# Turning v and the keys by 32x32 squares on VectorE and ScalarE instead of on TensorE, and spreading the gates' row by DMA

## The chip, the cores and the metric

The kernel runs on one core of one Trainium2 chip. The engines that matter here are TensorE (in the profile PE, with its weight loads as PEld), VectorE (DVE), ScalarE (ACT), GpSimd (POOL) and SyncE (SP), which issues most of the transfers. Each engine works through its own list of instructions in the order in which the program put them, and waits for the others by semaphores.

The metric is the device time of one execution in microseconds. The kernel before takes 1883.01 us as the median of three runs (1882.06 to 1885.18).

## What is computed

One decoder layer for 256 tokens of width 2048, in float32. Two token mixers run side by side and are merged by gates, then come a cross-attention into 256 memory tokens and a gated feed-forward part with a short causal convolution. Cut to the parts that matter here:

```
proj = h @ w_in                                   # all inputs of both mixers, and the gates
q, k, v, o, ir, fr = split(mlstm part)            # mLSTM: 4 heads, chunks of 64
r, kr, vr, wl, al, gl = split(rwkv part, shifted) # RWKV-7: 16 heads of 64

# mLSTM, per head: weights of token s for token t from the gates' running sums
b    = cumsum(logf);  dmat = b_t - b_s + i_s  (s <= t)
m_t  = max(b_t + m, max_s dmat);  dexp = exp(dmat - m_t)
s    = (q @ k.T) * dexp;  h = (s @ v) / max(|sum s|, exp(-m_t))

# RWKV-7, per head and token:
S = S * diag(w) - (S kk) (kk a).T + v k.T ;   y = S r

x = x + norm(merge(mLSTM, RWKV) @ w_out)
x = x + norm(cross_attention(norm(x), norm(mem)))
x = x + norm(gelu(conv(u)_gate) * conv(u)_up @ w_down)
```

## The kernel before

Most of the time goes into products of activations with weights that stream from memory. Each float32 weight chunk (128 x 1024 elements, 512 KB) is loaded by SP and split into a high part `wh` by ScalarE (line 410) and a low part `wl` by VectorE (line 432, `raw - wh`). Activations are split in the same way (`hh`, `hl`), and each product is three matrix instructions: high with high, high with low, low with high. They are all recorded by the helper `mm` at line 188. A block of kind "fm" gives features on the partitions and 256 tokens in the free dimension (results named `fm`); a block of kind "tm" gives tokens on the partitions (named `tm`). `wh` and `wl` have four buffers each, and the raw chunks three.

`run` (the loop over all blocks) writes the instruction lists by hand. While it emits the products of one chunk it calls `side.half()` after every half chunk, which is 12 products of an fm block. At each such step the class `Spread` lets side work emit one piece: first the evacuation of the last block (`bulk`), then background tasks (`back`), each only while a running budget for VectorE and ScalarE is positive, and then the chains, which emit a piece every so many steps (their `chain` number) whatever the bulk does. A generator's `yield` ends a piece, so an empty `yield` waits for one step. What is emitted earlier stands earlier in each engine's list.

The blocks come in this order: small weights and gates, r, k, v, q and k of the mLSTM, its v and o, the branch gates, the two branches, the mixer's output, the cross-attention, and the feed-forward part.

Three places are touched by the change.

**v.** `v_evac` (two blocks, `hf` 0 and 1) writes v with features on the partitions into `vT`. The recurrence also needs it with tokens on the partitions, in `vt`. After four empty steps TensorE turns four squares of 128x128 into a PSUM bank (line 939), ScalarE copies the bank to `vt`, and this happens twice per block. Then `start_rwkv` may start the recurrence, and `bonus(hf)` is added to the background tasks.

**Keys.** `rwkv(hf)` runs the recurrence for half of the heads in four chunks of 64 tokens. Both halves advance together, one piece every three steps. In the first three chunks TensorE turns four squares of the keys `BK` into a PSUM bank (line 981), and ScalarE copies the bank into `bkt`. `bkt` is read at the end of the chunk by the state's update (`Tn`). The pieces of a chunk are: the turning; the Gram products (`gram`) with two masks by VectorE; the inverse blocks and the copies of v; `lv1` and `X`; `lv2`; `U`; then `Tn` and `Y`. `inverses` is the background task that prepares `M["cmt"]` before the recurrence can start: Gram products (`gramA`) by TensorE and some sixty small VectorE operations.

**The gates' row.** `gates` computes the gates' running values with four heads on four partitions. One row of 256 values per head, `R[6]`, must be known on all 128 partitions. It is split into a high and a low part, and TensorE multiplies each with a column of the 4x4 identity `id4` into the PSUM tile `gbc`: two groups of four products, one per pair of heads. VectorE clamps the differences into `pw` (24 operations), and ScalarE takes the exponential.

`x_tokens`, much later, already turns the residual for the output by VectorE (32x32 squares) and ScalarE, in the way the change now uses for v.

Of the kernel before, what the change touches and what calls it, by code (L numbers as in the profile page):

```python
# [15 lines left out]
P = 128  # L16
# [136 lines left out]
def _layer(ctx, tc, nc, d, dbg):  # L153
# [12 lines left out]
    def T2(name, shape=None, dt=F32):  # L166
        return mp.tile(shape or [P, 2, S], dt, tag="T2", bufs=6, name=name)

# [43 lines left out]
    E2 = [slice(0, 64), slice(64, 128)]  # L212
    mhalf = cp.tile([P, 16], F32, name="mhalf")
    pool.memset(mhalf, -0.5)
# [359 lines left out]
    flip = [0]  # L574

    def PR():
        flip[0] += 1
        if flip[0] % 2:
            M["pr"] = C("pr", "bg1", [P, 2, 2, S])
        return M["pr"][:, 1 - flip[0] % 2]  # L580
# [73 lines left out]

    id4 = cp.tile([4, 4], F32R, name="id4")

    def gates():

        act.copy(id4, con[0:4, 0:4])
        RT = M["rows"]  # L660
# [72 lines left out]
        M["pw"] = pw  # L733
        g2 = T2("g2", dt=F32R)
        split(g2[0:4, 0], g2[0:4, 1], R[6])
        for _ in range(6):
            yield
        for h2 in range(2):
            q = aux("gbc", [P, 2, S])
            for j in range(2):  # L740
                sel = id4[:, h2 * 2 + j:h2 * 2 + j + 1].broadcast_to((4, P))
                mm(q[:, j], sel, g2[0:4, 0], stop=False)
                mm(q[:, j], sel, g2[0:4, 1], start=False)
            for j in range(2):
                h = h2 * 2 + j
                for (jt, dq), ci in CI.items():
                    o = jt * 256 + dq * 64 - jt * 128
                    dve.tensor_scalar(pw[:, h, o:o + 64], q[:, j, dq * 64:(dq + 1) * 64], cols[:, ci, h:h + 1], 0.0,
                                      op0=ALU.subtract, op1=ALU.max)
                yield  # L750
# [171 lines left out]
    def v_evac(hf):  # L922
        def gen(ps):
            if hf == 0:
                M["vT"], M["vt"] = U("vT"), U("vt", [P, 2, 1024])
            for g in range(2):
                p0 = hf * 4 + g * 2
                pr = PR()
                dve.tensor_mul(pr, ps[g], bc(st0.rb, 2))
                yield  # L930
                for j in range(2):
                    shiftmix(M["vT"][:, p0 + j], pr[:, j], 16 + p0 + j)
                yield
            for _ in range(4):
                yield
            for t in range(2):
                q = aux("vt", [P, 4, 128])
                for j in range(4):
                    pe.transpose(q[:, j], M["vT"][:, hf * 4 + j, t * P:(t + 1) * P], ident)
                act.copy(M["vt"][:, t, hf * 512:(hf + 1) * 512], q)  # L940
                yield
            M["v", hf] = True
            start_rwkv()
            tasks["bon", hf] = side.add(bonus(hf), back=True)
        return gen

    def bonus(hf):
# [11 lines left out]
    def rwkv(hf):  # L959
# [6 lines left out]
        def heads():  # L966
            for j in range(4):
                for e in range(2):
                    yield j, e

        ysb = None
        for c in range(4):
# [5 lines left out]
            if c < 3:  # L978
                q = aux("bkt", [P, 4, 128])
                for j in range(4):  # L980
                    pe.transpose(q[:, j], flat(BK[:, p0 + j, c]), ident)
                act.copy(bkt, q)
                yield
            au = C("au", f"au{hf}", [P, 2, 2, 4, 64])
# [4 lines left out]
            for e in range(2):  # L989
                dve.tensor_mul(ab[:, e], qs[e][:, :, 0:64], bc(sm, 4))  # L990
                dve.tensor_mul(gr[:, e], qs[e][:, :, 64:128], bc(im, 4))
                yield

# [6 lines left out]
            for e in range(2):  # L1000
                act.copy(uv[E2[1 - e], e], v[:, e])
            yield

# [9 lines left out]
            if c:  # L1013
# [651 lines left out]
    def x_tokens():  # L1665

        M["xt"] = []
        for f in range(4):
            if f % 2 == 0:
                M["xt"].append(U("xt", [P, 2, 1024]))  # L1670
            q = C("xq", f"au{f % 2}", [P, 4, 2, 4, 32])
            flat = q.rearrange("p k t b i -> p (k t b i)")
            for i in range(2):
                v = M["xr"][f // 2][:, f % 2 * 4 + i * 2:f % 2 * 4 + i * 2 + 2]
                dve.transpose(flat[:, i * 512:(i + 1) * 512], v.rearrange("p k s -> p (k s)"))
                yield
            o = M["xt"][f // 2][:, :, f % 2 * 512:f % 2 * 512 + 512].rearrange("p t (k b i) -> p t k b i", k=4, b=4)
            for b in range(4):
                for c in range(4):
                    act.copy(o[b * 32:b * 32 + 32, :, :, c], q[c * 32:c * 32 + 32, :, :, b].rearrange("p k t i -> p t k i"))  # L1680
                    if c % 2:
                        yield

# [157 lines left out]
```

## Time and profile before

| What | Value |
|---|---|
| median of three runs | 1883.01 us (1882.06 to 1885.18) |
| the profiled execution, its own time | 1882.86 us |
| its span from first to last instruction | 1881.1 us |
| TensorE busy | 1867.8 us, 99% |
| VectorE busy | 1313.9 us, 70% |
| ScalarE busy | 1035.0 us, 55% |
| granted TensorE clock | 0.997 over the span |
| transposes of v, on TensorE | 16, from 156.0 to 181.6 us |
| transposes of keys, on TensorE | 24, from 262.3 to 390.5 us |
| products of the gates' row | 8, from 83.4 to 87.5 us |

In a row of a group the figures after the bar are the busy time of all its instructions and the mean time of one in ns, and after the second bar the idle time of the engine before them. In a row of the timeline the first two figures are start and length in us, and equal neighbours are merged (x4). A matrix instruction's length is longer than the distance to the next one, because they are pipelined, so prices on TensorE are read from start to start. The profiled execution lies 1.8 us above its span.

### The profile page before, as it was taken

The numbers are of one execution on the slowest core, as the hardware profiler recorded it, in microseconds if no ns is written. First come the engines' busy times: TensorE is split into PE (matmuls) and PEld (weight loads), VectorE is DVE, ScalarE is ACT, GpSimd is POOL, SyncE is SP. The second block draws the span as 40 slices with busy tenths as digits, with TensorE's granted clock in tenths as the row PEclk, the third lists the DMA queues.
The fourth block names the chain that finished last, engine by engine and source line by source line (L and its number), as shares of the span: only waits on it lengthen the run. The fifth ranks groups of instructions, "written<-read, shape, count | busy, mean of one in ns | idle before, by whom it ended". The sixth has DMA issues, their size and how long they took to land.

```text
span 1881.1 us, 36660 instructions
## 1 busy us (share of the span) xinstructions
PE 1867.8 (99%) x15038; PEld 1774.5 (94%) x15038; DVE 1313.9 (70%) x1957; ACT 1035.0 (55%) x1619; POOL 30.6 (2%) x53
## 2 busy tenths in 40 slices
PE   9999999999999999999999999999999999999998
PEld 9999988999999999899999999999999998888886
DVE  6879985765765767777877666777666675556555
ACT  6677355554544655666565555564445555545453
POOL 0000000100100000000000000000000000000000
PEclk9999999999999999999999999999999999999999
DMA  7655554354556664545555566555655556555554
GB/s 252 196 175 181 167 177 146 110 175 146 182 175 206 237 234 163 176 163 180 197 196 192 199 194 198 194 191 191 195 198 193 196 191 216 195 192 196 193 190 154
DMA packets 97912, 352.73 MB, mean 188 GB/s; under 512 B 11056, under 2 KB 11312, under 8 KB 97360
## 3 DMA queue, kind: packets, MB, share of 16 engines
q1 hardware_dynamic: 96496, 348.07, 56.2%
q8 instruction: 117, 1.92, 0.4%
q0 software_dynamic: 384, 1.18, 0.3%
q10 hardware_dynamic: 864, 1.15, 0.2%
q14 instruction: 51, 0.42, 0.1%
HBM read 347.73 MB, written 2.10 MB: 186 GB/s over the span
## 4 chain that ended last, share of the span: by engine, by line
PE 95%; DVE 3%; issue 1%; ACT 1%; DMA 0%; POOL 0%; SPq 0%; DVEq 0%; POOLq 0%; ACTq 0%
PE fm L188 66%; PE tm L188 24%; DVE wl L432 1%; PE gram L188 0%; PE Y L188 0%; DVE ql L66 0%; ACT wh L410 0%; PE lv L188 0%; DMA wsm<-in_w_sm_dram 0%; DVE z L66 0%; PE num L188 0%; DVE hl L66 0%; PE X L188 0%; PE zwa L188 0%; PE U L188 0%
## 5 line engine op out<-in xcount | busy, mean ns | idle before, releaser
L432 DVE TENSOR_TENSOR wl<-raw,wh 128x1024 fp32r<-128x1024 f32 (+2 forms) x756 | 789.3, 1059 | 427.4 <-ACT wh L410 424.3
L410 ACT CAST wh<-raw 128x1024 fp32r<-128x1024 f32 (+2 forms) x756 | 679.8, 916 | 520.7 <-PE fm L188 335.0
L188 PE MATMUL fm<-fh,wl 128*128 128x256 f32 x2048 | 566.3, 277 | 0.5 <-DVE wl L432 0.4
L188 PE MATMUL fm<-fh,wh 128*128 128x256 f32 x2048 | 566.3, 277 | 0.1
L188 PE MATMUL fm<-fl,wh 128*128 128x256 f32 x2048 | 565.0, 276 | 0.0
L188 PEld LDWEIGHTS fm<-fh,wl 128*128 128x128 f32 x2048 | 385.0, 188 | 1.0 <-DVE wl L432 1.0
L188 PEld LDWEIGHTS fm<-fh,wh 128*128 128x128 f32 x2048 | 384.9, 188 | 0.4 <-ACT fh L66 0.4
L188 PEld LDWEIGHTS fm<-fl,wh 128*128 128x128 f32 x2048 | 384.5, 188 | 0.0
L188 PE MATMUL tm<-wh,as 128*128 128x512 f32 x1024 | 315.1, 389 | 0.0
L188 PE MATMUL fm<-hh,wh 128*128 128x256 f32 x1072 | 302.0, 282 | 1.4 <-ACT wh L421 1.4
L188 PE MATMUL fm<-hh,wl 128*128 128x256 f32 x1072 | 298.3, 278 | 0.1
L188 PE MATMUL fm<-hl,wh 128*128 128x256 f32 x1072 | 298.2, 278 | 0.0
L188 PEld LDWEIGHTS tm<-wh,as 128*128 128x128 f32 x1024 | 192.1, 188 | 39.8
L188 PEld LDWEIGHTS fm<-hh,wh 128*128 128x128 f32 x1072 | 202.4, 189 | 3.4 <-ACT hh L66 1.5
L188 PEld LDWEIGHTS fm<-hl,wh 128*128 128x128 f32 x1072 | 202.4, 189 | 0.2
L188 PEld LDWEIGHTS fm<-hh,wl 128*128 128x128 f32 x1072 | 202.3, 189 | 0.3 <-DVE wl L422 0.3
L188 PE MATMUL tm<-wl,as 128*128 128x512 f32 x512 | 199.2, 389 | 0.0
L188 PEld LDWEIGHTS tm<-wl,as 128*128 128x128 f32 x512 | 96.1, 188 | 20.0
L66 ACT CAST as<-ac 128x256 fp32r<-128x256 f32 x128 | 45.6, 404 | 113.5 <-PE tm L188 113.5
L66 DVE TENSOR_TENSOR as<-ac,as 128x256 fp32r<-128x256 f32 x128 | 48.6, 421 | 62.2 <-ACT as L66 62.2
L188 PE MATMUL fm<-mgh,wh 128*128 128x256 f32 x256 | 71.0, 277 | 0.0
L188 PE MATMUL fm<-mgh,wl 128*128 128x256 f32 x256 | 70.9, 277 | 0.0
(361 smaller groups left out, 2156.1 us busy)
## 6 DMA issues: line engine op xcount, KB each, us to landing
raw<-in_w_fu_dram SPq DMA_DIRECT2D x256, 512.0 KB, 4.2
raw<-in_w_in_dram SPq DMA_DIRECT2D x160, 512.0 KB, 3.7
raw<-in_w_fd_dram SPq DMA_DIRECT2D x128, 512.0 KB, 4.0
raw<-in_w_br_dram SPq DMA_DIRECT2D x32, 512.0 KB, 3.9
raw<-in_w_mo_dram SPq DMA_DIRECT2D x32, 512.0 KB, 4.1
raw<-in_w_xk_dram SPq DMA_DIRECT2D x8, 512.0 KB, 4.3
raw<-in_w_xq_dram SPq DMA_DIRECT2D x8, 512.0 KB, 3.6
raw<-in_w_xv_dram SPq DMA_DIRECT2D x8, 512.0 KB, 3.9
```

Of the source, the lines that this page charges most:

```text
L66: return f(out, *a, **k)
L188: pe.matmul(out, lhsT, rhs, start=start, stop=stop, skip_group_check=True)
L410: nc.scalar.copy(h, v)
L432: nc.vector.tensor_sub(l, v, h)
```

## The change

- v: `v_evac` ends after its shift and hands over to a new chain `v_tokens(hf)` (a piece every two steps). For each pair of feature tiles, VectorE transposes 128 x 512 elements in squares of 32x32 into a small tile `vq` (one instruction per pair), and ScalarE carries the squares to their places in `vt`: 16 copies of 32 partitions per pair, each with 128 elements per partition. `v_tokens` then marks v as ready, starts the recurrence if it may, and adds `bonus`.
- Keys: in each of the first three chunks, `keys` does the same for `BK`: one transpose of 128 x 512 by VectorE, then 16 copies by ScalarE. The transpose is emitted with the chunk's first piece. The copies follow three at a time per half in four pieces, and the rest at `lv2`. The piece that only did the turning is gone, so a chunk has one piece less.
- The gates' row: no split, no `id4` and no products. Four transfers on POOL's queue copy `R[6]` of each head from its one partition to 128 partitions of `gb` in SBUF. VectorE clamps from there, after eight empty steps instead of six.
- `x_tokens` uses the new helper `turned`, with the same instructions as before. The T2 tiles have seven buffers instead of six, and `mhalf` has 24 columns instead of 16.

```diff
-        return mp.tile(shape or [P, 2, S], dt, tag="T2", bufs=6, name=name)
+        return mp.tile(shape or [P, 2, S], dt, tag="T2", bufs=7, name=name)
...
-    mhalf = cp.tile([P, 16], F32, name="mhalf")
+    mhalf = cp.tile([P, 24], F32, name="mhalf")
...
+    def turned(q, v, o):
+        n = v.shape[1]
+        flat = q.rearrange("p k t b i -> p (k t b i)")
+        for k in range(0, n, 2):
+            dve.transpose(flat[:, k * S:(k + 2) * S], v[:, k:k + 2].rearrange("p k s -> p (k s)"))
+            yield
+        o = o.rearrange("p t (k b i) -> p t k b i", k=n, b=4)
+        for b in range(4):
+            for c in range(4):
+                act.copy(o[b * 32:b * 32 + 32, :, :, c], q[c * 32:c * 32 + 32, :, :, b].rearrange("p k t i -> p t k i"))
+                if c % 2:
+                    yield
...
-    id4 = cp.tile([4, 4], F32R, name="id4")
...
-        act.copy(id4, con[0:4, 0:4])
...
-        g2 = T2("g2", dt=F32R)
-        split(g2[0:4, 0], g2[0:4, 1], R[6])
-        for _ in range(6):
+        gb = C("gb", "au1", [P, 4, S])
+        for h in range(4):
+            pool.dma_start(gb[:, h], R[6][h:h + 1].unsqueeze(1).broadcast_to((1, P, S)))
+        for _ in range(8):
             yield
         for h2 in range(2):
-            q = aux("gbc", [P, 2, S])
-            for j in range(2):
-                sel = id4[:, h2 * 2 + j:h2 * 2 + j + 1].broadcast_to((4, P))
-                mm(q[:, j], sel, g2[0:4, 0], stop=False)
-                mm(q[:, j], sel, g2[0:4, 1], start=False)
...
-                    dve.tensor_scalar(pw[:, h, o:o + 64], q[:, j, dq * 64:(dq + 1) * 64], cols[:, ci, h:h + 1], 0.0,
+                    dve.tensor_scalar(pw[:, h, o:o + 64], gb[:, h, dq * 64:(dq + 1) * 64], cols[:, ci, h:h + 1], 0.0,
...
-            for _ in range(4):
-                yield
-            for t in range(2):
-                q = aux("vt", [P, 4, 128])
-                for j in range(4):
-                    pe.transpose(q[:, j], M["vT"][:, hf * 4 + j, t * P:(t + 1) * P], ident)
-                act.copy(M["vt"][:, t, hf * 512:(hf + 1) * 512], q)
-                yield
-            M["v", hf] = True
-            start_rwkv()
-            tasks["bon", hf] = side.add(bonus(hf), back=True)
+            side.add(v_tokens(hf), chain=2)
         return gen
+
+    def v_tokens(hf):
+        for p0 in (hf * 4, hf * 4 + 2):
+            yield from turned(T2("vq", [P, 2, 2, 4, 32]), M["vT"][:, p0:p0 + 2], M["vt"][:, :, p0 * P:p0 * P + 256])
+        M["v", hf] = True
+        start_rwkv()
+        tasks["bon", hf] = side.add(bonus(hf), back=True)
...
+        def keys(o, v):
+            q = T2("bq", [P, 4, 4, 32])
+            dve.transpose(q.rearrange("p j b i -> p j (b i)"), v.rearrange("p j s t -> p j (s t)"))
+            yield
+            for b in range(4):
+                for a in range(4):
+                    act.copy(o[b * 32:b * 32 + 32, :, a * 32:a * 32 + 32], q[a * 32:a * 32 + 32, :, b])
+                    yield
...
             if c < 3:
-                q = aux("bkt", [P, 4, 128])
-                for j in range(4):
-                    pe.transpose(q[:, j], flat(BK[:, p0 + j, c]), ident)
-                act.copy(bkt, q)
-                yield
+                turn = keys(bkt, BK[:, p0:p0 + 4, c])
+                next(turn)
+            else:
+                turn = iter(())
...
                 dve.tensor_mul(gr[:, e], qs[e][:, :, 64:128], bc(im, 4))
+                for _ in zip(range(3), turn):
+                    pass
                 yield
...
                 act.copy(uv[E2[1 - e], e], v[:, e])
+            for _ in zip(range(3), turn):
+                pass
             yield
...
                     dve.tensor_add(uv[E2[e], e], uv[E2[e], e], q[E2[e]])
+            for _ in zip(range(3), turn):
+                pass
             yield
...
                 dve.tensor_copy(mt[r, :, 32:64], q[r])
+            for _ in turn:
+                pass
             yield
```

More of the change, by code (lines that the diff above doesn't have):

```diff
@@ L1671, in x_tokens @@
             q = C("xq", f"au{f % 2}", [P, 4, 2, 4, 32])
[L1672 to L1675, printed above, removed]
+            v = M["xr"][f // 2][:, f % 2 * 4:f % 2 * 4 + 4]
+            o = M["xt"][f // 2][:, :, f % 2 * 512:f % 2 * 512 + 512]
+            for _ in turned(q, v, o):
                 yield
[L1677 to L1682, printed above, removed]
     def load_gain():
```

## The prediction

> **What bounds the kernel.** I read the page's parts 1, 2 and 4 first, then TensorE's waits, then the timeline around each operation that the change removes, and last the lead that VectorE has over TensorE in that stretch. From the page, and from the view of the waits (who waited for whom: us, times, longest):
>
> ```profile
> span 1881.1 us, 36660 instructions
> PE 1867.8 (99%) x15038; PEld 1774.5 (94%) x15038; DVE 1313.9 (70%) x1957; ACT 1035.0 (55%) x1619; POOL 30.6 (2%) x53
> ...
> PE 95%; DVE 3%; issue 1%; ACT 1%; DMA 0%; POOL 0%; SPq 0%; DVEq 0%; POOLq 0%; ACTq 0%
> ...
> PE fm L188 <- ACT wh L421: 1.4, 1, 1.4
> ...
> PE fm L188 <- DVE wl L432: 0.4, 1, 0.4
> ```
>
> TensorE is busy 99% of the span, is 95% of the chain that ended last, and waits for other engines some microseconds in all. So a microsecond taken off TensorE's queue is a microsecond off the kernel, provided that no engine that feeds it becomes late.
>
> **What TensorE loses.** The products go out one every 0.113 us in the feature-major blocks (155.82, 155.93 below) and one every 0.227 us in the token-major ones. Timeline of TensorE at a group of each kind that the change removes:
>
> ```profile
> 155.82 0.28 PE L188 MATMUL fm<-hl,wh 128*128 128x256 f32 x1
> 155.93 0.28 PE L188 MATMUL fm<-hh,wl 128*128 128x256 f32 x1
> 156.05 0.60 PE L939 MATMUL vt<-con,vT 128*128 128x128 f32 x4
> 156.41 0.37 PE L188 MATMUL fm<-hh,wh 128*128 128x256 f32 x1
> 156.62 0.28 PE L188 MATMUL fm<-hl,wh 128*128 128x256 f32 x1
> ```
>
> ```profile
> 262.31 0.39 PE L188 MATMUL tm<-wl,hh 128*128 128x512 f32 x1
> 262.55 1.03 PE L981 MATMUL bkt<-con,BK 128*128 128x128 f32 x8
> 263.33 0.48 PE L188 MATMUL tm<-wh,hh 128*128 128x512 f32 x1
> 263.65 0.40 PE L188 MATMUL tm<-wh,hl 128*128 128x512 f32 x1
> ```
>
> ```profile
> 83.20 0.28 PE L188 MATMUL fm<-hh,wl 128*128 128x256 f32 x1
> 83.41 0.74 PE L188 MATMUL gbc<-g,id 4*128 4x256 f32 x4
> 84.08 0.39 PE L188 MATMUL fm<-hh,wh 128*128 128x256 f32 x1
> 84.30 0.28 PE L188 MATMUL fm<-hl,wh 128*128 128x256 f32 x1
> ```
>
> ```profile
> L981 PE MATMUL bkt<-con,BK 128*128 128x128 f32 x24 | 3.1, 272 | 0.0
> ...
> L939 PE MATMUL vt<-con,vT 128*128 128x128 f32 x16 | 2.4, 273 | 0.0
> ...
> L188 PE MATMUL gbc<-g,id 4*128 4x256 f32 x8 | 1.5, 303 | 0.0
> ```
>
> The price of a group is the time from the product before it to the second product after it, less two steps. Four squares of v: 156.62 - 155.93 - 2 x 0.113 = 0.46, and 16/4 = 4 groups give 1.85. Eight squares of keys: 263.65 - 262.31 - 2 x 0.227 = 0.89, and 24/8 = 3 groups give 2.67. Four products of the gates' row: 84.30 - 83.20 - 2 x 0.113 = 0.87, and 2 groups give 1.75. Together **6.3 us** leave TensorE, all on the path.
>
> **What the other engines gain.** Groups with their shapes (busy, mean ns of one):
>
> ```profile
> L66 DVE STREAM_TRANSPOSE xq<-xr 128x512 f32<-128x512 f32 x8 | 5.6, 704 | 0.0
> ...
> L66 DVE TENSOR_SCALAR pw<-gbc,cols 128x64 f32<-128x64 f32 x24 | 4.8, 279 | 0.0
> ```
>
> ```profile
> L66 ACT COPY xt<-xq 32x256 f32<-32x256 f32 x64 | 25.8, 403 | 1.0
> ...
> L66 ACT ACT_TABLE_LOAD x4 | 5.1, 1283 | 2.9 <-PEq L1833 1.7 <-DVE tg L66 1.3
> ...
> L66 ACT COPY bg<-bkt 128x512 f32<-128x512 f32 x6 | 3.2, 588 | 2.4 <-PE bkt L981 2.3
> ...
> L66 ACT COPY vt<-vt 128x512 f32<-128x512 f32 x4 | 2.4, 588 | 3.4 <-PE vt L939 3.4
> L66 ACT COPY m<-lv 128x128 f32<-128x128 f32 x8 | 2.1, 265 | 5.3 <-PE lv L188 5.1
> ```
>
> VectorE: four transposes of 128x512 for v, six for the keys, at 704 ns: 7.0 us. Its 24 clamps of the gates change their source from PSUM to SBUF; I count them at the same 279 ns.
>
> ScalarE: 4 x 16 + 6 x 16 = 160 copies of 32 partitions x 128 elements. No row has that shape. Below it lies 0.265 us (m, as many elements, PSUM to SBUF), above it 0.403 us (xt, the same helper's copies with twice the elements). I take 0.30, since the difference of those two is mostly 128 more elements. 160 x 0.30 = 48 us, less the ten evacuations that go (10 x 0.588 = 5.9): about 42 us more on an engine that is busy 55%. The order of the changed program also holds nine table loads instead of seven, as the gates' exponentials now fall between two groups of sigmoids: 2 x 1.28 = 2.6 us more. The keys are wanted within their chunk, v only when the inverses are done. `x_tokens` issues through the new helper what it issued before; the seventh T2 buffer, the wider `mhalf` and the missing `id4` move small tiles only, and the order shows the products on the same operands: nothing for these.
>
> [...] By the rows, four squares cost 0.46 us of TensorE and 0.588 of ScalarE before, and 0.70 of VectorE and 16 x 0.30 = 4.8 of ScalarE after. [...] By the rows the freed engine is the one that bounds, and the sum starts from the 6.3 us.
>
> **VectorE's lead, where v is turned.** Busy time by stretch (PE, PEld, DVE, ACT, POOL, clock, DMA share, GB/s), then two weights' low parts and the products that first use them:
>
> ```profile
> 150.00:200.00 50.00, 50.00 (x459) 49.80 (x458) 46.66 (x73) 33.62 (x55) 6.46 (x8) 1.00 0.56 178
> 200.00:250.00 50.00, 50.00 (x371) 44.25 (x371) 45.44 (x81) 18.19 (x19) 0.00 (x0) 1.00 0.53 169
> 250.00:300.00 50.00, 50.00 (x367) 41.17 (x365) 36.06 (x61) 28.84 (x40) 0.00 (x0) 1.00 0.52 160
> ```
>
> ```profile
> 219.13 1.22 DVE L432 TENSOR_TENSOR wl<-raw,wh 128x1024 fp32r<-128x1024 f32 x1
> ...
> 224.91 0.39 PE L188 MATMUL tm<-wl,hh 128*128 128x512 f32 x1
> ```
>
> ```profile
> 259.13 1.23 DVE L432 TENSOR_TENSOR wl<-raw,wh 128x1024 fp32r<-128x1024 f32 x1 [0.70 <-ACT wh L410]
> ...
> 263.88 0.39 PE L188 MATMUL tm<-wl,hh 128*128 128x512 f32 x1
> ```
>
> VectorE is idle for only 7.9 of the 100 us from 150 to 250. The two tiles are ready 224.91 - 220.35 = 4.6 us and 263.88 - 260.36 = 3.5 us ahead of their use; every weight tile stands in VectorE's queue behind whatever was issued before it. In the changed program the order shows the second pair of head sums 72 and 48 products earlier, and the inverses' first Gram products 48 products earlier (1488 instead of 1536), which is 48 x 0.113 = 5.4 us: the four waiting steps of `v_evac` and its two transposing ones are gone, so the background work behind it comes sooner. Adding the row's mean of each VectorE instruction in program order from 150 us on, after has 5.0 us more ahead of the first tile (2.8 of it the four transposes, the rest inverse work that comes earlier) and 4.3 us more ahead of the second, and TensorE comes 1.85 us sooner to both. That is 6.9 against a lead of 4.6, and 6.2 against 3.5. So the wait is bounded by 0 below, if the work fits into the idle time (2.8 + 1.85 = 4.7 of 7.9), and by about 3 above (6.2 - 3.5 = 2.7), if none of it does. The idle time lies in small pieces that a queue with a backlog can use, and half of it lies behind the first tile; I take the middle, **1.5 us**.
>
> **ScalarE in the recurrence.** A chunk of `rwkv` puts six copies into each of four steps, 6 x 0.30 = 1.8 us, and eight into the last. The step's own work of 3.1 us and its one and a half casts of weights add up to 6.5 us at the fullest step, against some 6.3 us that TensorE has there. Behind the copies stand the evacuations of X and U, for which TensorE waits one step later. Below: 0 (21 of 50 us are idle from 250 to 300). Above: half a microsecond at four steps in three chunks, 6. The row is near the lower end, since ScalarE's backlog is gone after each step; I take **0.5**. One step less in three chunks lets the recurrence end some 70 products earlier; nothing waits for its end, so I count it at nothing.
>
> **The gates' row.** The four copies go to POOL's queue ahead of the two of `uh`.
>
> ```profile
> 60.00:110.00 50.00, 50.00 (x423) 48.51 (x422) 42.61 (x96) 31.99 (x57) 5.20 (x11) 1.00 0.66 196
> ```
>
> ```profile
> 67.73 0.48 POOL L691 COPY rows<-rows 4x64 f32<-4x64 f32 x1 [0.23 <-DVE rows L66]
> ```
>
> ```profile
> uh<-uh POOLq DMA_DIRECT2D x2, 256.0 KB, 4.4
> ```
>
> The row is complete before POOL's last copy ends at 68.2; the first clamp comes at about 85, the last at 89. With all four in flight they land in 4.4 us, at 73; one behind the other in 17.6, at 85.8. Either way in time; I count them at nothing, by the cover of those 17 us. Without that cover VectorE stands still with the weights' low parts behind it, and the copies of `uh`, for which TensorE's `zwa` products wait, come late too. The two table loads more sit where ScalarE is idle for 18 of 50 us (60 to 110 us) and lie under that.
>
> **Sum.** 1882.86 (the profiled execution: the span of 1881.1 and 1.8 around it) - 6.3 + 1.5 + 0.5 = **1878.6 us**, 0.23% less. The median of the three runs is 1883.01, 0.15 above the profiled execution, which changes nothing.
>
> **Rivals.** (1) Nothing is given back: VectorE's idle pieces take it all up, and ScalarE is never late. 1876.6. For it: almost no wait in before. Against it: the 4.6 and 3.5 us of lead.
> (2) Nearly all is given back: VectorE late by the full 3 us, and direct waits of TensorE on it (the head sums' low half, the scores) and on ScalarE cost 2 more. 1881.6, no change that can be told. For it: 92% busy and the work bunched. Against it: it uses none of the idle time.
> [...] If a copy of 32 partitions costs p and each step is full, 3 chunks x 4 steps x 6 copies x (p - 0.30) is TensorE's wait; it eats the gain from p = 0.39 on, and at 0.50 it is 14 us: 1891. For it: xt's 0.403, and 6.5 us of work in a step of 6.3. Against it: half of xt's elements, and idle time between the steps.
> That the change does not do what it says is no rival here: the changed order has 48 matrix instructions fewer.
>
> **Chances.** Forecast (1877.6 to 1879.8) 0.45, rival 1 0.16, rival 2 0.28, rival 3 0.11. A difference of 0.2%, 3.8 us, is about what the spread of the three runs (1882.06 to 1885.18) can tell from nothing. Rival 1 and the better four fifths of the forecast are past it: faster 0.52; the rest of the forecast and rival 2 lie within: 0.37; slower 0.11. The range from rival 1 less half a microsecond to just above rival 2: 1876.0 to 1883.2, leaving out rival 3 and some of both ends.
>
> **What would show it.** Right: no `vt`, `bkt` or `gbc` rows on PE; 0.46, 0.89 and 0.87 us less at those places; waits of PE for DVE `wl` of 1 to 2 us between 180 and 265 us; transposes at 0.70 and copies at 0.30 us; the clamps not waiting for the four copies. Wrong: waits of PE on DVE or ACT above 3 us in 180 to 420, copies above 0.39, a wait of DVE at the clamps, or another pace of the products (0.113) after 530 us, where the programs are alike.

## The result, and the profile after

The changed kernel takes 1899.76 us (median of 5 runs, 1899.44 to 1902.89), the kernel before in the same session 1883.28 (5 runs, 1882.06 to 1885.18). The ratio is 1.0089, 95% interval 1.0074 to 1.0104. That is slower by 16.5 us, outside the predicted range of 1876.0 to 1883.2 and far from 1878.6. The profiled execution has a span of 1898.0 us against 1881.1.

The page of the changed kernel: span, busy time of the engines, granted clock in 40 slices, and the chain by engine:

```profile
span 1898.0 us, 36752 instructions
...
PE 1865.7 (98%) x14990; PEld 1769.9 (93%) x14990; DVE 1318.2 (69%) x1966; ACT 1078.7 (57%) x1769; POOL 34.5 (2%) x57
...
PEclk9899999999999999999999999999999999999999
...
PE 88%; DVE 5%; ACT 3%; DMA 2%; issue 2%; POOL 0%; DVEq 0%; POOLq 0%; SPq 0%; ACTq 0%
```

TensorE's busy time fell by 2.1 us, but the chain lies on it for 88% of the span in place of 95%, and the second slice (47 to 95 us) shows a lowered clock. The waits of TensorE in the changed kernel (sum, times, longest):

```profile
PE fm L188 <- ACT wh L410: 10.6, 1, 10.6
PE fm L188 <- DVE wl L432: 2.4, 3, 1.5
PE zwa L188 <- ACT lw L66: 1.6, 2, 1.2
```

One wait of 10.6 us, for the high part of a weight chunk, is the largest thing new. Stretches of the changed kernel around it (PE, PEld, DVE, ACT, POOL busy, then granted clock, DMA share, GB/s):

```profile
66.00:70.00 4.00, 4.00 (x38) 4.00 (x37) 3.97 (x14) 1.14 (x2) 2.50 (x5) 1.00 0.90 119
70.00:75.00 5.00, 5.00 (x47) 4.85 (x46) 1.60 (x3) 0.00 (x0) 0.00 (x0) 1.00 0.99 33
75.00:80.00 5.00, 3.73 (x33) 3.52 (x31) 0.00 (x0) 0.00 (x0) 0.00 (x0) 1.00 0.99 51
80.00:85.00 5.00, 0.00 (x0) 0.00 (x0) 0.00 (x0) 0.00 (x0) 0.00 (x0) 0.88 1.00 83
85.00:90.00 5.00, 0.72 (x2) 0.50 (x2) 0.74 (x1) 1.82 (x3) 0.00 (x0) 0.50 0.68 235
```

The kernel before at the same place:

```profile
70.00:75.00 5.00, 5.00 (x47) 4.84 (x46) 4.20 (x10) 2.58 (x5) 0.00 (x0) 1.00 0.70 209
```

The last two columns tell it: from 70 to 85 us the DMA engines are busy all the time and move 33 to 83 GB/s, where before they moved 209 at a share of 0.70. All engines then run dry. What the DMA engines were busy with stands in the rows of the gates' row, of SP's loads and of ScalarE's next cast:

```profile
L748 POOL DMA_DIRECT2D gb<-rows x4: 536/542/740, 66.2 to 68.0; - x4
...
DMA to landing us min/median/max: 7.1/14.3/19.6
```

```profile
L363 SPq DMA_DIRECT2D raw<-in_w_in_dram x8: 327/328/12492, 60.1 to 97.5; - x8
...
DMA to landing us min/median/max: 3.6/4.8/20.4
```

```profile
88.18 1.04 ACT L410 CAST wh<-raw 128x1024 fp32r<-128x1024 f32 x1 [19.18 <-DMA raw<-in_w_in_dram]
```

The four row transfers are issued from 66.2 to 68.0 us and land one after another, the last 19.6 us after its issue. A weight load issued among them, at 67.7 us, lands 20.4 us later (the median is 4.8), and ScalarE, which must cast that weight, waits 19.18 us for it. SP needs 12.49 us for the issue of a later load (0.33 is usual). When TensorE starts again, its products stand 0.21 us apart and not 0.113, at a granted clock of 0.50:

```profile
89.28 0.58 PE L188 MATMUL fm<-hh,wh 128*128 128x256 f32 x1 [10.55 <-ACT wh L410]
...
91.13 0.41 PE L188 MATMUL fm<-hl,wh 128*128 128x256 f32 x1
91.34 0.41 PE L188 MATMUL fm<-hh,wl 128*128 128x256 f32 x1
```

### The profile page after: what moved, and what is told of

Its sections match the earlier page's. It is cut to its first block, busy times and chain, and to the rows that moved or that the text cites. A ratio compares the mean times of both kernels' runs of the same rounds, so it can differ in the third digit from the quotient of the medians.

```text
span 1898.0 us, 36752 instructions
## 1 busy us (share of the span) xinstructions
PE 1865.7 (98%) x14990; PEld 1769.9 (93%) x14990; DVE 1318.2 (69%) x1966; ACT 1078.7 (57%) x1769; POOL 34.5 (2%) x57
## 4 chain that ended last, share of the span: by engine, by line
PE 88%; DVE 5%; ACT 3%; DMA 2%; issue 2%; POOL 0%; DVEq 0%; POOLq 0%; SPq 0%; ACTq 0%
PE fm L188 62%; PE tm L188 23%; DVE wl L432 2%; DMA raw<-in_w_in_dram 2%; ACT wh L410 1%; ACT bg L66 0%; PE Y L188 0%; PE num L188 0%; PE gram L188 0%; DVE BK L66 0%; PE X L188 0%; DMA wsm<-in_w_sm_dram 0%; DVE tmp L66 0%; DVE vT L66 0%; PE lv L188 0%
## 5 line engine op out<-in xcount | busy, mean ns | idle before, releaser
L188 PE MATMUL fm<-hh,wh 128*128 128x256 f32 x1072 | 302.4, 282 | 11.8 <-ACT wh L410 10.6
```

Source lines behind the costliest of these rows:

```text
L188: pe.matmul(out, lhsT, rhs, start=start, stop=stop, skip_group_check=True)
```

## The experiments

Times are medians; the kernel before had 1882.63 to 1883.62 in these sessions. To place a difference inside the span, I use five marks that lie at the same point of the weights' stream in all kernels: the first product of `gcol` (the gates' columns: 73 us, ahead of the first place where TensorE's times part), of the first `zwa` group (the products behind the decays `lw`: 92), of the first `ssk` group (head sums: 130), of the last `sc` group (the mLSTM's scores: 232), and the load of the 185th streamed chunk (596, behind the recurrence). The table shows how much later (or earlier, negative) than in the kernel before each mark comes, in us, less the same difference at `gcol`; each is worked out from start times in the traces, so it belongs to the one profiled execution of a kernel and not to the median (of the row only, of the row only in two steps with 6 turns, and of the keys only it was the longest of the runs). Behind the last mark the programs are alike, and the difference still wanders there, by -1.1 to +2.4 us.

| Kernel | median us | ratio, 95% interval | zwa | ssk | sc | 185th load |
|---|---|---|---|---|---|---|
| the change | 1899.76 | 1.0089 (1.0074 to 1.0104) | +11.7 | +15.7 | +16.7 | +18.7 |
| row only | 1900.41 | 1.0094 (1.0080 to 1.0107) | +10.7 | +17.6 | +17.0 | +17.2 |
| row only, 6 turns | 1895.10 | 1.0061 (1.0047 to 1.0074) | +10.9 | +10.9 | +10.3 | +10.4 |
| row only, two steps | 1883.75 | 1.0000 (0.9991 to 1.0009) | -1.8 | -0.6 | -1.2 | -0.9 |
| row only, two steps, 6 turns | 1880.44 | 0.9984 (0.9975 to 0.9993) | -1.8 | -1.8 | -2.4 | -2.2 |
| v and keys turned, row on TensorE | 1886.63 | 1.0018 (1.0009 to 1.0027) | 0.0 | 0.0 | +1.1 | +2.1 |
| v only | 1886.25 | 1.0015 (1.0006 to 1.0023) | 0.0 | 0.0 | +1.0 | +1.1 |
| keys only | 1891.13 | 1.0042 (1.0030 to 1.0054) | 0.0 | 0.0 | 0.0 | +8.3 |

### Which part makes the loss

First theory: the row's transfers make nearly all of it. Rival: the turned squares do, by ScalarE's copies and VectorE's lateness. Two kernels split the change.

The changed kernel with the row back on TensorE:

```diff
-        gb = C("gb", "au1", [P, 4, S])
-        for h in range(4):
-            pool.dma_start(gb[:, h], R[6][h:h + 1].unsqueeze(1).broadcast_to((1, P, S)))
-        for _ in range(8):
+        g2 = T2("g2", dt=F32R)
+        split(g2[0:4, 0], g2[0:4, 1], R[6])
+        for _ in range(6):
...
+                mm(q[:, j], sel, g2[0:4, 0], stop=False)
+                mm(q[:, j], sel, g2[0:4, 1], start=False)
```

> The changed kernel with the gates' row back on TensorE (the one-hot products, their split and the identity of 4); v and the keys stay turned by VectorE and ScalarE. Theory 1 (the four transfers of the gates' row read one partition 128 times each, fill the DMA engines from 66 to 85 us, the weights land late and TensorE stops 10.7 us at 78 us, after which its clock is lowered for a while): the stop is gone, no lowered clock behind 80 us, and the time falls by 10.7 + about 3 for the clock less the 1.75 us that the products cost, to about 1888 us; what is left above the kernel before, some 4 us, is what the turned squares cost. Theory 2 (the copies on ScalarE and the later VectorE are the main loss): about 1898 us, and the waits of TensorE between 195 and 420 us keep their sums.

The kernel before with the row alone changed:

```diff
-        g2 = T2("g2", dt=F32R)
-        split(g2[0:4, 0], g2[0:4, 1], R[6])
-        for _ in range(6):
+        gb = C("gb", "au1", [P, 4, S])
+        for h in range(4):
+            pool.dma_start(gb[:, h], R[6][h:h + 1].unsqueeze(1).broadcast_to((1, P, S)))
+        for _ in range(8):
...
-                mm(q[:, j], sel, g2[0:4, 0], stop=False)
-                mm(q[:, j], sel, g2[0:4, 1], start=False)
```

> The kernel before with the gates' row alone moved to the four transfers; v and the keys are still transposed by TensorE. Theory 1: the idle stretch of TensorE near 78 us and the lowered clock are all there, 12 us over the kernel before, about 1895 us. Theory 2: the transfers are harmless, 1.75 us saved, about 1881.5 us.

Without the row's transfers 1886.63 us, with them alone 1900.41. The row carries the loss, and more than I had expected of it: 17.5 us alone, not 12. The rival has a part of 3.7 us, where a gain was forecast. The parts do not add up: 17.5 and 3.7 make 21.2, and the change costs 16.5. By the marks 2.9 us of the difference lie between `zwa` and `ssk`, where the row alone loses 6.9 and the change 4.0; that place is taken up below.

### What is slow in the row's transfers

Three kernels change the source, the number of reads of the gates' four partitions, and the queue.

The changed kernel with the source in DRAM:

```diff
-            pool.dma_start(gb[:, h], R[6][h:h + 1].unsqueeze(1).broadcast_to((1, P, S)))
+            pool.dma_start(gb[:, h], d["w_up"][h:h + 1, 0:S].partition_broadcast(P))
```

> The changed kernel, with the four transfers taking their row from a tensor in DRAM (the first four rows of w_up's first 256 columns) in place of the four partitions of SBUF that hold the gates' row: same queue, same issue place, same bytes and same destination, so the gates' factors are computed from other numbers. Theory 1a (the slow part is the reading of one SBUF partition by all 16 DMA engines): the transfers land in about 5 us each, the weights' transfers keep their pace, no stop at 78 us, about 1886 us. Theory 1b (the slow part is the software queue or the writing of 512 pieces of 1 KB): landing near 14 us as now, and about 1899 us.

The changed kernel with the row in two steps:

```diff
-            pool.dma_start(gb[:, h], R[6][h:h + 1].unsqueeze(1).broadcast_to((1, P, S)))
+            pool.dma_start(gb[0:P:4, h], R[6][h:h + 1].unsqueeze(1).broadcast_to((1, 32, S)))
+        for i in range(1, 4):
+            pool.dma_start(gb[i:P:4], gb[0:P:4])
```

> The changed kernel, with each row spread first to 32 partitions (every fourth one), and three more transfers from those 32 to the partitions beside them: 128 KB are read from the gates' four partitions, not 512 KB. Theory 1a: the slow reading lasts a quarter as long, some 5 us in place of 19, the three raw buffers of the weights cover it, no stop at 78 us, and the time is that of the changed kernel less 14 us, about 1886 us. Theory 1b: as many pieces are written on the same queue, and more transfers are issued, so the stop stays, 1899 us or above.

The changed kernel with the transfers on ScalarE's queue:

```diff
-            pool.dma_start(gb[:, h], R[6][h:h + 1].unsqueeze(1).broadcast_to((1, P, S)))
+            act.dma_start(gb[:, h], R[6][h:h + 1].unsqueeze(1).broadcast_to((1, P, S)))
```

> The changed kernel with the four transfers of the gates' row issued by ScalarE on a hardware queue in place of POOL's software queue; source, destination and bytes are the same. If the reading of one partition is what is slow: the stop at 78 us stays, about 1899 us, the transfers take 14 us or more to land. If the software queue is what is slow: no stop, about 1886 us.

From DRAM 1887.46 us (ratio 1.0021, 1.0012 to 1.0030), in two steps 1885.76 (1.0013, 1.0004 to 1.0022), on ScalarE's hardware queue 1898.90 (1.0081, 1.0064 to 1.0099). The row transfers, from DRAM:

```profile
L748 POOL DMA_DIRECT2D gb<-in_w_up_dram x4: 536/542/740, 66.7 to 68.5; - x4
...
DMA to landing us min/median/max: 3.6/4.5/6.1
```

From SBUF on the hardware queue:

```profile
L748 ACTq DMA_DIRECT2D gb<-rows x4: 551/1269/5445, 74.2 to 77.4; - x4
...
DMA to landing us min/median/max: 8.1/14.5/20.1
```

In two steps, a stretch of the span as above:

```profile
70.00:75.00 5.00, 5.00 (x47) 4.84 (x46) 1.89 (x4) 1.53 (x3) 1.22 (x3) 1.00 0.87 333
```

Same bytes, pieces and queue from DRAM: 4.5 us to landing in place of 14.3, and no stop. The other queue with the old source: 14.5 us, and the stop is back (its place and its waiter differ: the issue on ScalarE came later, and `uh`'s copies, behind it, held the `zwa` products for 7.3 us). With a quarter of the reads the DMA engines move 333 GB/s from 70 to 75 us, and TensorE doesn't stop. So the slow thing is the reading of these four partitions of SBUF, 128 times each, by all DMA engines: 512 KB took from 66.2 to 87.6 us (68.0 + 19.6). Why that reading is slow, these runs don't settle; none reads four other partitions.

### The second half of the row's cost

Row only cost 17.5 us, and 6.9 of them (from +10.7 to +17.6) arise between the first `zwa` and the first `ssk`, long after the transfers have landed. ScalarE there, in the kernel with the row only:

```profile
119.94 1.28 ACT L66 ACT_TABLE_LOAD   x1
121.23 0.84 ACT L66 ACTIVATE lw<-zwa,par 128x256 f32<-128x256 f32 x2
```

With 8 empty turns (the empty `yield`s ahead of the clamps) the exponentials of `pw` fall between two pairs of `lw`. ScalarE then loads its table twice more, `lw` comes late, and TensorE's `zwa` products, which need the bank, wait. In this kernel:

```profile
PE zwa L188 <- ACT lw L66: 2.9, 2, 1.7
```

The two waits, 2.9 us in all, are followed by another stretch at a clock of 0.50 (from 124 us on, for 6.8 us). A kernel with the row alone in two steps still had the 8 turns:

```diff
-            pool.dma_start(gb[:, h], R[6][h:h + 1].unsqueeze(1).broadcast_to((1, P, S)))
+            pool.dma_start(gb[0:P:4, h], R[6][h:h + 1].unsqueeze(1).broadcast_to((1, 32, S)))
+        for i in range(1, 4):
+            pool.dma_start(gb[i:P:4], gb[0:P:4])
```

> The kernel before with the gates' row alone moved to transfers, in two steps (first to every fourth partition, then from those 32 to the three beside each). With the four rows read 32 times and not 128 times the weights keep their pace, and the two groups of one-hot products, 0.887 us each, are gone: 1.8 us under the kernel before, about 1881.2 us. If some of the stop is left (a short gap near 75 us, or a late row at the clamps), 1883 or above.

Two more, of the row in two steps and of the row as changed, have 6:

```diff
-        for _ in range(8):
+        for _ in range(6):
             yield
```

> The kernel before with the gates' row alone moved to transfers in two steps, as before, and the clamps two turns of the planner earlier (6 empty turns, as with the one-hot products, in place of 8). With 8 turns ScalarE's four exponentials of pw came between the second and the third pair of lw and cost two more table loads, and TensorE's zwa products waited 0.9 us for lw. Theory C (the 8 turns put them there): 7 table loads in all, no wait of zwa for lw, and 1.8 + 0.2 us (the drains behind the two groups) under the kernel before: about 1881 us against 1882.6. Rival: the order stays, 1883 to 1884 us.

> The kernel before with the gates' row alone moved, read 128 times from the four partitions as in the change, and 6 empty turns in place of 8. Theory C: the stop of some 10 us at 78 us and the lowered clock behind it stay, but the second lowered clock, near 125 us, is gone with the wait of zwa for lw: 12 us over the kernel before, about 1895 us, where 8 turns gave 1900.4. Rival (the transfers alone make all of it, whatever the order on ScalarE): about 1900 us.

1883.75, 1880.44 and 1895.10 us. With 6 turns the two table loads are gone. The groups of them that the turns change, in two steps with 8 turns, and then with 6:

```profile
L66 ACT ACT_TABLE_LOAD x6 | 7.7, 1283 | 3.0 <-PEq L1828 1.7 <-DVE tg L66 1.3
```

```profile
L66 ACT ACT_TABLE_LOAD x4 | 5.1, 1283 | 3.0 <-PEq L1828 1.7 <-DVE tg L66 1.3
```

The same 6 turns take 5.3 us off the row alone and 3.3 off the row in two steps, by medians of different sessions; at the `ssk` mark they are worth 6.7 and 1.2 (in two steps the wait was 0.9 us and the clock stayed up). So the row as changed has two faults, and both are now shown: some 12.7 us are the stop and the clock behind it (+10.9 at `zwa`, and the saving of 1.8 eaten), and some 5 the order on ScalarE. With both mended the row by itself gains: ratio 0.9984 (0.9975 to 0.9993), 1.8 us at the mark right behind it. It is the only kernel here that beats the kernel before; its gain lies just within the 0.2% that I had set as what can be told. Of the 0.2 us more that the expectation added for drains behind the groups, no run shows anything.

### v and the keys

v alone turned is the kernel with both turned (row on TensorE), with the keys back on TensorE:

```diff
-                turn = keys(bkt, BK[:, p0:p0 + 4, c])
-                next(turn)
...
+                q = aux("bkt", [P, 4, 128])
+                for j in range(4):
+                    pe.transpose(q[:, j], flat(BK[:, p0 + j, c]), ident)
+                act.copy(bkt, q)
+                yield
```

> Only v is turned by VectorE and carried by ScalarE; the keys and the gates' row are left to TensorE. TensorE saves 4 x 0.46 = 1.85 us. Theory A (the loss of the turned squares lies at v, where the four turns and 64 copies make the weights' halves late between 150 and 265 us; the kernel with both turned had two gaps of 1.06 and 0.68 us at 184 and 221 us): about 2 us over the kernel before, near 1885. Theory B (it lies in the recurrence, with the keys): 1 to 2 us under the kernel before, near 1881.5.

The keys alone turned have v back there instead:

```diff
-            side.add(v_tokens(hf), chain=2)
+            for _ in range(4):
+                yield
+            for t in range(2):
+                q = aux("vt", [P, 4, 128])
+                for j in range(4):
+                    pe.transpose(q[:, j], M["vT"][:, hf * 4 + j, t * P:(t + 1) * P], ident)
+                act.copy(M["vt"][:, t, hf * 512:(hf + 1) * 512], q)
+                yield
...
```

> Only the keys are turned; v and the gates' row are left to TensorE. TensorE saves 3 x 0.89 = 2.7 us. Theory A: what the recurrence gives back is less than that, 1 to 2 us under the kernel before, near 1881.5. Theory B (96 copies of 0.296 us in the recurrence hold up ScalarE's other copies there, the groups of lv, X, U, Tn and Y wait, and 4 us more are spent in them, as in the kernel with both turned): about 2 us over, near 1885.

v alone 1886.25, the keys alone 1891.13. Both theories fell halfway: each part loses, and the two losses, some 3.6 and 8.5 us, do not add up to the 3.7 of both together. TensorE's waits with v alone, 150 to 265 us:

```profile
PE fm L188 <- DVE wl L432: 0.9, 1, 0.9
PE tm L188 <- DVE wl L432: 0.5, 1, 0.5
```

VectorE in the same kernel, ahead of the first of them (the product stood until 185.5):

```profile
181.12 0.70 DVE L66 STREAM_TRANSPOSE vq<-vT 128x512 f32<-128x512 f32 x1
181.75 2.55 DVE L66 TENSOR_TENSOR BK<-kt 64x512 f32<-64x512 f32 x4
184.33 1.29 DVE L432 TENSOR_TENSOR wl<-raw,wh 128x896 fp32r<-128x896 f32 x2
```

With the keys alone, TensorE's waits from 260 to 530 us, stretches around the longest, and ScalarE ahead of it:

```profile
PE X L188 <- ACT m L66: 2.9, 3, 1.7
PE lv L188 <- DVE m L66: 2.4, 1, 2.4
```

```profile
398.00:402.00 4.00, 1.57 (x45) 1.51 (x46) 2.81 (x6) 3.87 (x11) 0.00 (x0) 0.83 0.54 165
402.00:406.00 4.00, 3.57 (x61) 3.31 (x57) 2.13 (x4) 3.84 (x12) 0.00 (x0) 0.50 0.31 99
```

```profile
392.54 1.84 ACT L66 COPY bg<-bq 32x128 f32<-32x128 f32 x6
394.41 1.05 ACT L410 CAST wh<-raw 128x1024 fp32r<-128x1024 f32 x1
397.35 0.63 ACT L66 ACTIVATE sg<-sg 128x512 f32<-128x512 f32 x1 [1.89 <-DVE sg L66]
397.89 1.12 ACT L410 CAST wh<-raw 128x896 fp32r<-128x896 f32 x2
```

TensorE stands for 2.4 us from 398.1 on, and then the clock is halved. ScalarE was not simply full: six copies of the keys stand ahead of a cast, VectorE waits 2.31 us for that cast, its `sg` comes late, and ScalarE then waits 1.89 us for `sg`. The next cast, the next `wl` and, behind it on VectorE, the `m` that TensorE needs all come late. So I asked whether the 16 copies make the stops, and whether it is their place that matters.

The keys alone, with one copy per chunk:

```diff
-            for b in range(4):
-                for a in range(4):
-                    act.copy(o[b * 32:b * 32 + 32, :, a * 32:a * 32 + 32], q[a * 32:a * 32 + 32, :, b])
-                    yield
+            act.copy(o, q.rearrange("p j b i -> p j (b i)"))
+            yield
```

> The kernel with the keys alone turned, with one ScalarE copy of 128x512 for each chunk in place of the 16 copies of 32x128, so that the squares are not carried to their places and the recurrence works on keys in a wrong order; the transposes by VectorE stay. Theory D (the 16 copies, 4.7 us of ScalarE for each chunk of each half, hold up the copies of m, X and the weights' halves, TensorE stops for over 2 us and its clock is lowered): the waits of X and lv between 260 and 530 us fall under 1.5 us in sum, no lowered clock there, and the time is 1 to 3 us under the kernel before, about 1881. Rival E (the order of the recurrence, shifted by TensorE's missing transposes, or VectorE's turns, is what costs): as with the 16 copies, about 1891 us.

The keys alone with all their copies, and one empty turn (in a second kernel two) ahead of the recurrence:

```diff
+        for _ in range(1):
+            yield
         ysb = None
```

> The keys alone turned, with one empty turn ahead of the recurrence's first step, so that all its steps fall one place later beside the other work. Theory H (the loss hangs on where the 16 copies fall beside m, X and the weights' halves): the time moves by several us, to anywhere between 1882 and 1891. Rival (the copies cost the same wherever they fall): 1890 to 1892 us.

> As with one empty turn, with two. Theory H: another time again, between 1882 and 1891 us. Rival: 1890 to 1892 us.

With one copy in place of sixteen 1883.18 us (ratio 1.0001, 0.9993 to 1.0010). The loss is gone, as Theory D said, but not the gain of 1 to 3 us that it forecast, and one wait of 260 to 530 us is longer than it allowed:

```profile
PE X L188 <- ACT m L66: 1.7, 1, 1.7
```

It is the second of the two long stops of the keys alone: the same group, at 436 us here and at 445 there, in the last chunk, where no keys are turned, and well after the last of the 96 copies (412.6 us). So the copies do not make that stop. What is left for it is the changed order of the pieces, one of Rival E's two causes; with the pieces one or two places later, below, it is gone. Behind it the clock fell with the 16 copies and not with one.

But with all sixteen copies and the steps one or two places later, 1884.38 (1.0004, 0.9995 to 1.0013) and 1884.53 (1.0009, 1.0000 to 1.0018). TensorE's waits with one turn, 260 to 530 us:

```profile
PE X L188 <- ACT m L66: 1.1, 1, 1.1
PE Y L188 <- DVE ha L66: 0.7, 1, 0.7
```

So most of the 8 us of the keys alone were a matter of place: in an unlucky one the copies stop TensorE for 2.4 us and the order of the pieces for 1.7, and the clock does the rest; in a lucky one they cost about what TensorE saves. The trace bears the size out: its stops there make 5.4 us, and 10.2 us at half the clock cost some 5.1 more (an estimate: half of it); less the 2.7 saved that is 7.8, against 8.3 at the mark. One step or two made no difference to the time, so Theory H's "another time again" failed, though with two the longest wait lay elsewhere (1.8 us, at `lv`). No place that I tried gained, nor did the turned keys without their copies: TensorE's 2.7 us come out whole in no run.

v alone, with one copy in place of 16 for each pair of feature tiles:

```diff
-            yield from turned(T2("vq", [P, 2, 2, 4, 32]), M["vT"][:, p0:p0 + 2], M["vt"][:, :, p0 * P:p0 * P + 256])
+            q = T2("vq", [P, 2, 2, 4, 32])
+            dve.transpose(q.rearrange("p k t b i -> p (k t b i)"), M["vT"][:, p0:p0 + 2].rearrange("p k s -> p (k s)"))
+            yield
+            act.copy(M["vt"][:, :, p0 * P:p0 * P + 256], q.rearrange("p k t b i -> p t k (b i)"))
+            for _ in range(8):
+                yield
```

> v alone turned, but with one transpose of 128x1024 on VectorE and one ScalarE copy of the same bytes for each pair of channel tiles in place of two transposes and 16 copies of 32x128; v's squares are not carried to their places, so the recurrence works on a v in a wrong order. Theory F (VectorE's late halves of the weights are the loss: at 184 us the product waited 1.04 us for a wl that stood behind a transpose and four BK products): the waits for wl stay and the time stays near 1885 to 1886 us. Theory G (ScalarE's 64 copies are the loss): the waits for wl go, about 1881 us.

1883.67 us (0.9999, 0.9990 to 1.0007), between the two theories. VectorE's turns are the same in both kernels, four of 128x512 (the expectation's 128x1024 in place of two transposes is not what the edit does). With 16 copies, and then with one:

```profile
L66 DVE STREAM_TRANSPOSE vq<-vT x4: 697/704/705, 155.8 to 235.2; 128x512 f32<-128x512 f32 x4
```

```profile
L66 DVE STREAM_TRANSPOSE vq<-vT x4: 702/705/705, 155.8 to 231.5; 128x512 f32<-128x512 f32 x4
```

The wait of 0.9 us for `wl` is gone, the later one of 0.4 stays, and the `sc` mark comes 0.5 us early in place of 1.0 late. VectorE's own waits for `wh`, 150 to 265 us, with the 16 copies, and then with one:

```profile
DVE wl L432 <- ACT wh L410: 5.4, 9, 1.2
```

```profile
DVE wl L432 <- ACT wh L410: 3.2, 4, 1.2
```

So v's loss, in this place, is ScalarE's copies: they make `wh`, and through it `wl`, late, and without them 1.5 us come back at the `sc` mark with VectorE's turns unchanged. The rest, 1.3 of the 1.85 us that TensorE saves, is missing with one copy too; whether the turns or the changed order take it isn't told apart.

### The changed kernel mended

```diff
-            pool.dma_start(gb[:, h], R[6][h:h + 1].unsqueeze(1).broadcast_to((1, P, S)))
-        for _ in range(8):
+            pool.dma_start(gb[0:P:4, h], R[6][h:h + 1].unsqueeze(1).broadcast_to((1, 32, S)))
+        for i in range(1, 4):
+            pool.dma_start(gb[i:P:4], gb[0:P:4])
+        for _ in range(6):
```

> The changed kernel with both faults of the row taken away: two steps of transfer and 6 empty turns. The row then saves some 2 to 3 us, the turned squares cost some 3 us (v and keys turned, row on TensorE: 1886.6 against 1882.9). If the parts add: 1883 to 1885 us, no faster than the kernel before. If the turned squares gain once the gates' work stands where it stood: under 1881 us.

1883.88 us, ratio 1.0001 (0.9993 to 1.0010). The row's gain and the turned squares' loss cancel. The mended row without the turned squares stays ahead of it.

## Why the prediction was wrong, point by point

- **What TensorE loses: right for the row, not shown for the rest.** The transposes and the products are gone, and the row's 1.75 us show as 1.8 at the `zwa` mark when nothing else goes wrong. The 1.85 of v and the 2.67 of the keys never came out whole at a mark, not even with one copy in place of 16 (0.5 us early at `sc` for v, 0.0 at the 185th load for the keys).
- **The gates' row, "I count them at nothing, by the cover of those 17 us": this step failed.** Its arithmetic was not far off: one behind the other, 17.6 us, where the last row landed 21.4 us after the first issue. But I asked only whether the row itself lands in time for the clamps and who stands behind it on POOL. I didn't ask what else the same DMA engines have to carry in those 17 us: the weights, on SP's queue. What of them was in hand lasted TensorE for 12.5 us, from the first issue at 66.2 to the end of its last product at 78.7, and not for the 23 us that passed until the next weight was cast (89.2). The listed sign, "a wait of DVE at the clamps", was thus the wrong place to look. (The clamps were put at 85 to 89 us; they stood at 88.3 to 93.9 in the kernel before and at 104.9 to 109.8 in the changed one.) The price of 4.4 us came from `uh`, whose source is spread over 64 partitions; this one's lies on one. The failed step cost about 12.7 us.
- **The two table loads, "lie under that": failed.** I counted ScalarE's idle time over 50 us; what mattered was that they stand ahead of `lw`, which frees the bank for `zwa`. In the change TensorE waits 1.6 us there and loses clock after it: about 4 us between `zwa` and `ssk` (+11.7 to +15.7).
- **VectorE's lead, taken 1.5 of 0 to 3: right in place, but not the whole.** The waits for `wl` came where expected. v gave back 1.85 + 1.0 = 2.9 us, the upper end; with one copy in place of 16 it gave back 1.85 - 0.5 = 1.3, near the 1.5. The other 1.5 are ScalarE's copies at v, which the working put at nothing.
- **ScalarE in the recurrence, taken 0.5 of 0 to 6: size wrong.** In the kernel with v and the keys turned, 1.0 is lost behind `sc` where 2.67 was to be saved: 3.7 given back. What the copies and the order took in the recurrence depended on place: with the keys alone 8.3 + 2.7 = 11 us, beyond the 6 of the range. The price of a copy was right; groups of the changed kernel:

```profile
L66 ACT COPY bg<-bq 32x128 f32<-32x128 f32 x96 | 28.4, 296 | 7.4 <-DVE bq L66 6.1
...
L66 DVE TENSOR_SCALAR pw<-gb,cols 128x64 f32<-128x64 f32 x24 | 4.1, 249 | 0.0
```

  The reasoning "ScalarE's backlog is gone after each step" was an average over steps; a single step that isn't clear costs 1 to 2 us, and the halved clock behind it, 6.8 and 3.4 us long in the keys alone, may double that (an estimate: half of such a stretch is lost).
- **The rivals.** Without the row the result is beyond rival 2 (nearly all given back): 1886.6, where it had 1881.6, or 1883.3 with the row's 1.75 back. More was given back than the 4.5 us that TensorE saved there. The slower rival named 0.39 us per copy as the point from which the gain is gone, and they take 0.296; TensorE stopped in the recurrence all the same, in the keys alone (2.4 and 1.7 us). With v and the keys turned on TensorE the kernel was the faster: 1882.63 us, where v alone turned the new way took 1886.25 and the keys alone 1891.13.
- VectorE's busy time rose by 4.3 us, not 7.0; the clamps from SBUF take 249 ns, not 279, which is 0.7 of it, and the row's split, 0.4, is gone. The rest I haven't followed.

## What to carry to other kernels

A small transfer is not cheap because its bytes are few: ask from how many partitions it reads, and whose transfers wait meanwhile. Here 512 KB read from four partitions took 21.4 us, and a weight load issued among them landed after 20.4, where the same bytes from DRAM landed in 4.5 us per transfer. The row went out better in two steps, first to every fourth partition: no stop, and 1.8 us gained at the `zwa` mark. And when work is moved to engines off the critical path, check the order in which each engine's list gets it, not only the idle share: here two empty turns cost 3 to 5 us, and one shift of the recurrence was worth nearly 7.

## What the runs showed of the hardware

TensorE's granted clock fell to one half not only behind the stop of 10.6 us but behind stops of about 2 us. Each lowered stretch between 60 and 530 us lasted about 3.4, 6.8 or 10.2 us: 10.24 and 3.41 in the change (from 83.8 and 124.7 us on), 6.8 with the row alone (from 124 us on) and with the keys alone (from 400.7 us on). By TensorE's waits and gaps in that part of these traces, no single stop of up to 1.5 us was followed by it (the longest in the change, 1.49 us at 199 us, was not); of those between 1.5 and 1.7 us some were (1.6 us for `X` on the hardware queue and in the mended kernel, 1.7 us for `X` with the keys alone) and some not (1.7 us for `X` with one copy for the keys); and five longer ones were (1.8 us with the keys two steps later, 1.95 in two steps, some 2.0 with the row from DRAM, 2.1 on the hardware queue, 2.4 with the keys alone). It also fell behind two pairs of stops (0.47 and 1.17 us in the change, 1.71 and 1.17 with the row alone), and not behind a third (0.79 and 0.75, on the hardware queue). A stop of 1.95 us at 184 us, in the kernel with the row in two steps and v and keys turned:

```profile
184.00:188.00 4.00, 2.13 (x15) 2.13 (x16) 3.97 (x8) 2.19 (x5) 0.00 (x0) 0.91 0.26 50
188.00:192.00 4.00, 4.00 (x26) 4.00 (x25) 4.00 (x7) 3.39 (x6) 0.97 (x2) 0.66 0.72 225
```

The length of a stop does not decide it alone. Later in the span, with v alone turned, a stop of 2.14 us left the clock at 1.00:

```profile
773.47 1.13 PE L188 MATMUL xsc<-kT,qT 128*128 128x256 f32 x4 [2.14 <-DVE qT L66]
```

```profile
774.00:776.00 2.00, 2.00 (x10) 1.68 (x9) 1.97 (x5) 0.07 (x1) 0.00 (x0) 1.00 0.66 240
```

And behind a stop of 0.55 us that both the kernel before (at 821.9 us) and the changed kernel (at 839.7) have, the clock fell in the kernel before, for 3.41 us from 823.4 on, and not in the changed one. The kernel before there:

```profile
824.00:826.00 2.00, 1.87 (x9) 1.58 (x9) 1.79 (x6) 1.02 (x2) 0.00 (x0) 0.50 0.00 0
```

A lowered stretch of 3.41 us costs at most 1.7 us (an estimate: half of it), so differences of that size between single traces can be this alone.

Why some stops of one length were followed by a lowered clock and others not, these runs don't settle.
